# Products over channels: one stream's whole sum, then the other's, in a two-layer diffusion block

## The chip, the cores and the metric

The program runs on one core of a Trainium2 chip. The metric is device time in microseconds (us) of one execution. Engines are named PE (TensorE, matrix products; PEld is its load of the stationary operand), DVE (VectorE), ACT (ScalarE), POOL (GpSimd) and SP (SyncE, which here only issues DMAs).

## The reference, cut to what matters

Two layers act on 512 latent tokens and 256 context tokens, 1024 channels each. Context tokens share all weights. In the last layer only the latent tokens go on behind the mixers. Cut from the reference:

```python
for l in range(DEPTH):                                   # 2 layers
    h_lat = _modulate(_rms_norm(x_lat, norm1_g[l]), m_lat[0], m_lat[1])    # h_ctx likewise
    proj = jnp.concatenate([h_ctx, h_lat], axis=1) @ w_in[l]               # one projection for all mixers
    ya_l = _conformer_conv(a_l, ...)                     # 31 taps over tokens, layer norm, silu
    yb_l = _neighbourhood_attention(qb_l, kb_l, vb_l, kb_c, vb_c, rpb[l], rows)   # 8 heads of 64
    yc_l, yc_c = _gated_deltanet(...)                    # two directions, chunks of 64
    # merge: z = sigmoid(ga)*(ya@w_br[0]) + sigmoid(gb)*(yb@w_br[1]) + sigmoid(gc)*(yc@w_br[2]); z @ w_out
    x_lat = x_lat + m_lat[2][:, None, :] * _merge(mg_l, ya_l, yb_l, yc_l, w_branch[l], w_out[l])
    # feed-forward: (silu(gate) * val) @ w_down, gate and val = 3-tap conv of h @ w_up, 2 x 2816 wide
    x_lat = x_lat + m_lat[5][:, None, :] * _conv_ffn(h2_lat, ffn_up[l], ...)
    # x_ctx the same, in the first layer only
```

## The kernel before

**Operands.** Activations lie channel-major: eight tiles of 128 channels, with 512 columns for the latent stream ("l") and 256 for the context ("c"). Each value is split into a rounded part and the rest, so a stream has tile pairs `hl`/`ol` (latent) and `hc`/`oc` (context). A weight is split the same way in `wunit` (L126 to L133): a DMA on SP's queue brings `raw`, ACT casts it to `whi` (L131), DVE subtracts to get `wlo` (L132). A product over 1024 channels has eight steps k, and in each step three terms: `hl` by `whi`, `ol` by `whi`, `hl` by `wlo` (and the same for the context). So a latent result is a sum of 24 instructions of 512 columns in one PSUM bank, a context result one of 24 instructions of 256 columns in another.

**Two routines issue these products.** `mm_b` (L143 to L154) issues a whole sum at once. It serves the projections before the DeltaNet (`proj_b`, L475; tiles `pjl`, `pjc`), the branch products of the merge (L1281; `mbl`, `mbc`), the output projection (L1321; `wo`, one stream a call), and in the feed-forward the up products (`up_mm`, L1434; `upl`, `upc`) and the down products (L1390; `dn` for both streams). In its loops the streams are innermost: for each k and each term first the latent product, then the context product, so 512 and 256 columns alternate. The first three up units of the first layer call it stream by stream, because the latent half of the normalised input is ready before the context's, and so do the down products of the last part of that layer.

`mm_gen` (L442 to L449) issues the same products as a generator, with the same alternation, and after each k gives a number: the microseconds that it accounts for what it issued, 3 x 768 / 2400 = 0.96 with both streams. Units made from it (the gate projections, whose results `mg_units` turns into `mge` by a tanh on ACT at L1125, and the projections of the convolution, `conv_a_proj`) wait in a queue, with those of the attention's projections (`na`, L584, 0.33 a step) and of the convolution's layer norm.

**What sets the order.** `fill(us)` (L426 to L440) takes the queue's units from the front and steps them until the sum of the numbers that they give has reached `us`:

```python
while us > 0 and (q or self.live):
    if self.live is None:
        self.live = q.popleft()
        ...
    try:
        us -= next(self.live)
```

It is called in the DeltaNet (its chunk products, the block inverse, the scan and its output) and in the attention, with constants for each place and layer: in the first layer `fill(2.1)` behind each step of the attention, and `fill(2.5)` behind each step that prepares its operands. The step that reaches the sum is issued whole. What is left in the queue behind the attention is issued in `finish` (L404). Each unit loads and splits the next unit's weights when it begins. Beneath this, a scheduler of the framework sets the order of instructions on each engine from their dependencies, so the order on PE is not that of the code throughout.

**Stages**, with the starts that the trace shows for the first layer: projections before the DeltaNet (about 99 us), its chunk products (first `kk` at 212), block inverse, scan, the second direction (366), the transposes of its output (`oT`, L1016, last at 508; ACT copies them to `oev`, L1018, and a DMA writes `yc`), the attention's operands (loads `ax`, L1148, transposes `aT`, L1154), its jobs (536 to 698: scores `sc`, softmax on DVE and ACT, transposed probabilities `PT`, L1218, values `yl`/`yc`, L1233) with the convolution's taps (`ca`, L519) on DVE beside them, the rest of the queue (698 to 770), merge, output projection, feed-forward (953 to 1516). The second layer follows with the same stages; its queue's units and everything behind the mixers have one stream only.

Of the kernel before, what the change touches and what calls it, by code (L numbers as in the profile page):

```python
# [64 lines left out]
class Net:  # L65
# [76 lines left out]

    def mm_b(self, outs, w, xs, then={}):  # L143

        n = len(xs[0])
        for k in range(n):
            wk = w(k)
            for i, (a, b) in enumerate(((0, 0), (0, 1), (1, 0))):
                for o, x in zip(outs, xs):
                    self.nc.tensor.matmul(o, wk[a], x[k][b], start=(k == 0 and i == 0), stop=(k == n - 1 and i == 2))  # L150
            if k in then:
                then[k]()

    def pair_tiles(self, s, k):  # L154
        n = NL if s == "l" else NX
# [284 lines left out]
                self.live = None  # L440

    def mm_gen(self, outs, w, xs):  # L442
        n, t = len(xs[0]), sum(o.free_size() for o in outs) * 3 / 2400
        for k in range(n):
            wk = w(k)
            for i, (a, b) in enumerate(((0, 0), (0, 1), (1, 0))):
                for o, x in zip(outs, xs):
                    self.nc.tensor.matmul(o, wk[a], x[k][b], start=(k == 0 and i == 0), stop=(k == n - 1 and i == 2))  # L448
            yield t  # L449

    def proj_gen(self, src, both):
        hi, lo = self.wunit(src, 1024)
# [1078 lines left out]
```

## Time and profile before

| | before |
|---|---|
| median of 3 runs | 2596.06 us (2586.71 to 2603.39) |
| profiled execution | 2594.31 us, its span 2592.5 us |
| busy share of the span | PE 96%, PEld 83%, DVE 71%, ACT 41%, POOL 0% |
| mean granted clock of PE | 0.983 |

The profile is of one execution, which took 2594.31 us; its span, first to last instruction, is 2592.5 us. Busy shares are averages over stages with different limits. A product's row has its own duration; consecutive products overlap, so how fast they are issued is read from the differences of their starts.

### The profile page before, as it was taken

How to read it: one execution, taken by the hardware profiler on the slowest of the kernel's cores; microseconds unless marked ns; L12 is line 12 of the kernel's file. 1: busy time of each engine (PE TensorE's matmuls, PEld its weight loads, DVE VectorE, ACT ScalarE, POOL GpSimd, SP SyncE). 2: the span in 40 equal slices, each digit the busy share in tenths (PEclk: the TensorE clock that was granted, in tenths of full speed). 3: DMA queues.
4: the chain of work that ended last, by engine and by line, in shares of the span. 5: the costliest groups of instructions: out<-in, count | busy, mean ns of one | idle time of the engine just before them, and what ended most of it. 6: DMA issues, size and time to landing. Idle time of an engine off the chain costs nothing. (4 is left out here: it accounts for less than half of the span.)

```text
span 2592.5 us, 42262 instructions
## 1 busy us (share of the span) xinstructions
PE 2494.4 (96%) x16079; PEld 2156.6 (83%) x16079; DVE 1851.6 (71%) x4138; ACT 1067.5 (41%) x2159; POOL 8.4 (0%) x32
## 2 busy tenths in 40 slices
PE   6999999989999999999999999998989999999999
PEld 4889898967778888888888898887877778888887
DVE  6675578789679888776656477776768977755463
ACT  4564343445342244223223355634344543533242
POOL 0000000000000000000000000000000000000000
PEclk9999999999999999999999989998999999999999
DMA  7224434353458554453442342343446376322332
GB/s 253 91 76 137 138 99 140 98 177 109 149 186 270 179 176 125 121 161 115 150 135 87 110 141 95 120 134 112 146 125 211 100 251 188 130 90 98 98 98 90
DMA packets 207276, 356.77 MB, mean 138 GB/s; under 512 B 54832, under 2 KB 103200, under 8 KB 206944
## 3 DMA queue, kind: packets, MB, share of 16 engines
q1 hardware_dynamic: 182176, 320.97, 39.3%
q10 hardware_dynamic: 24896, 33.09, 3.6%
q8 instruction: 127, 2.08, 0.3%
q14 instruction: 77, 0.63, 0.1%
HBM read 297.31 MB, written 56.68 MB: 137 GB/s over the span
## 5 line engine op out<-in xcount | busy, mean ns | idle before, releaser
L132 DVE TENSOR_TENSOR wlo<-raw,whi 128x1024 fp32r<-128x1024 f32 (+2 forms) x319 | 385.4, 1209 | 292.3 <-ACT whi L131 289.1
L131 ACT CAST whi<-raw 128x1024 fp32r<-128x1024 f32 (+2 forms) x319 | 331.8, 1041 | 616.2 <-PE dn L150 197.7
L150 PE MATMUL upl<-hl,whi 128*128 128x512 f32 (+1 forms) x728 | 282.4, 389 | 2.4 <-ACT hl L322 1.9
L150 PE MATMUL upl<-ol,whi 128*128 128x512 f32 (+1 forms) x728 | 282.1, 388 | 0.0
L150 PE MATMUL upl<-hl,wlo 128*128 128x512 f32 (+1 forms) x728 | 280.9, 386 | 0.2 <-DVE wlo L132 0.2
L448 PE MATMUL pjl<-hl,whi 128*128 128x512 f32 x512 | 210.6, 411 | 7.6 <-ACT whi L131 7.6
L519 DVE SCALAR_TENSOR_TENSOR ca<-yp,caw,ca 128x783 f32<-128x783 f32 (+1 forms) x240 | 212.9, 887 | 6.7 <-ACT ca L512 4.6
L448 PE MATMUL pjl<-ol,whi 128*128 128x512 f32 x512 | 206.6, 404 | 0.0
L448 PE MATMUL pjl<-hl,wlo 128*128 128x512 f32 x512 | 206.2, 403 | 0.3 <-DVE wlo L132 0.2
L150 PEld LDWEIGHTS upl<-hl,whi 128*128 128x128 f32 x728 | 137.3, 189 | 30.7 <-ACT hl L322 2.1
L150 PEld LDWEIGHTS upl<-ol,whi 128*128 128x128 f32 x728 | 137.5, 189 | 30.0
L150 PEld LDWEIGHTS upl<-hl,wlo 128*128 128x128 f32 x728 | 137.4, 189 | 30.1 <-DVE wlo L132 0.7
L150 PE MATMUL dn<-fll,whi 128*128 128x512 f32 x352 | 139.0, 395 | 0.0
L150 PE MATMUL dn<-fhl,wlo 128*128 128x512 f32 x352 | 139.0, 395 | 0.0
L150 PE MATMUL dn<-fhl,whi 128*128 128x512 f32 x352 | 138.6, 395 | 0.1
L448 PEld LDWEIGHTS pjl<-hl,whi 128*128 128x128 f32 x512 | 97.8, 191 | 29.5 <-ACT whi L131 9.7
L448 PEld LDWEIGHTS pjl<-hl,wlo 128*128 128x128 f32 x512 | 97.6, 191 | 21.6 <-DVE wlo L132 1.2
L448 PEld LDWEIGHTS pjl<-ol,whi 128*128 128x128 f32 x512 | 98.0, 191 | 18.9 <-issue 0.5
L245 DVE CUSTOM_DVE_ANT_1 aj<-at,crows,par 128x512 f32<-128x512 f32 x128 | 93.1, 747 | 27.7 <-DMA at<-ada_t 16.0
L584 PE MATMUL na<-wlo,hl 128*128 128x256 f32 x384 | 108.9, 284 | 0.6 <-DVE wlo L132 0.6
L584 PE MATMUL na<-whi,hl 128*128 128x256 f32 x384 | 109.1, 285 | 0.0
L584 PE MATMUL na<-whi,ol 128*128 128x256 f32 x384 | 109.1, 284 | 0.0
(405 smaller groups left out, 6450.3 us busy)
## 6 DMA issues: line engine op xcount, KB each, us to landing
raw<-w_b SPq DMA_DIRECT2D x88, 512.0 KB
raw<-f_up SPq DMA_DIRECT2D x88, 512.0 KB
at<-ada_t SPq DMA_DIRECT2D x160, 256.0 KB
raw<-w_o SPq DMA_DIRECT2D x32, 512.0 KB
raw<-f_dn SPq DMA_DIRECT2D x32, 448.0 KB
raw<-w_a SPq DMA_DIRECT2D x24, 512.0 KB
mg<-mge ACTq DMA_DIRECT2D x48, 256.0 KB
raw<-w_br SPq DMA_DIRECT2D x24, 512.0 KB
```

What stands on the lines that cost most here:

```text
L131: self.nc.scalar.copy(hi[:, :n], r[:, :n])
L132: self.split = self.nc.vector.tensor_sub(lo[:, :n], r[:, :n], hi[:, :n]).ins
L150: self.nc.tensor.matmul(o, wk[a], x[k][b], start=(k == 0 and i == 0), stop=(k == n - 1 and i == 2))
L245: V.tensor_tensor_reduce(p, w, self.crows[:, r, 4 * h:4 * h + 4], 1.0, m if h else self.p(l, "adab")[:, t:t + 1], ALU.mult, ALU.add, accum ...
L448: self.nc.tensor.matmul(o, wk[a], x[k][b], start=(k == 0 and i == 0), stop=(k == n - 1 and i == 2))
L519: nc.vector.scalar_tensor_tensor(a, y[:, k:k + n], w[:, 31 * c + k:31 * c + k + 1], a, ALU.mult, ALU.add)
L584: self.nc.tensor.matmul(ps[:, :256], x[k][a], wk[b], start=(k == 0 and j == 0), stop=(k == 7 and j == 2))
```

## The change

`mm_b` puts the stream outermost: all k and all terms of the first stream, then all of the second; what hangs behind a step (`then`) is done in the last stream. `mm_gen` does the same, and gives its number after each k of one stream: 3 x 512 / 2400 = 0.64 for a latent step, 0.32 for a context step. A new routine, `mm_k`, holds the three products of a step, so that all these rows have one line, L154. `fill`, its constants and all callers stay.

```diff
     def mm_b(self, outs, w, xs, then={}):
 
-        n = len(xs[0])
-        for k in range(n):
-            wk = w(k)
-            for i, (a, b) in enumerate(((0, 0), (0, 1), (1, 0))):
-                for o, x in zip(outs, xs):
-                    self.nc.tensor.matmul(o, wk[a], x[k][b], start=(k == 0 and i == 0), stop=(k == n - 1 and i == 2))
-            if k in then:
-                then[k]()
+
+        for s in range(len(xs)):
+            for k in range(len(xs[s])):
+                self.mm_k(outs[s], w(k), xs[s], k)
+                if s == len(xs) - 1 and k in then:
+                    then[k]()
+
+    def mm_k(self, o, wk, x, k):
+        for i, (a, b) in enumerate(((0, 0), (0, 1), (1, 0))):
+            self.nc.tensor.matmul(o, wk[a], x[k][b], start=(k == 0 and i == 0), stop=(k == len(x) - 1 and i == 2))
 
     def mm_gen(self, outs, w, xs):
-        n, t = len(xs[0]), sum(o.free_size() for o in outs) * 3 / 2400
-        for k in range(n):
-            wk = w(k)
-            for i, (a, b) in enumerate(((0, 0), (0, 1), (1, 0))):
-                for o, x in zip(outs, xs):
-                    self.nc.tensor.matmul(o, wk[a], x[k][b], start=(k == 0 and i == 0), stop=(k == n - 1 and i == 2))
-            yield t
+        for o, x in zip(outs, xs):
+            for k in range(len(x)):
+                self.mm_k(o, w(k), x, k)
+                yield o.free_size() * 3 / 2400
```

**PE, an up unit of the first layer.** The program's order of PE before, the start of a unit (buffer numbers count the tiles of the stream, one pair for each k):

```order
L150 MATMUL upl<-hl_9933,whi 128x512
L150 MATMUL upc<-hc_9949,whi 128x256
L150 MATMUL upl<-ol_9934,whi 128x512
L150 MATMUL upc<-oc_9950,whi 128x256
L150 MATMUL upl<-hl_9933,wlo 128x512
L150 MATMUL upc<-hc_9949,wlo 128x256
L150 MATMUL upl<-hl_9935,whi 128x512
```

and of the change, the end of one unit and the start of the next:

```order
L154 MATMUL upc<-hc_10011,whi 128x256
L154 MATMUL upc<-oc_10012,whi 128x256
L154 MATMUL upc<-hc_10011,wlo 128x256
L154 MATMUL upl<-hl_9981,whi 128x512
L154 MATMUL upl<-ol_9982,whi 128x512
L154 MATMUL upl<-hl_9981,wlo 128x512
L154 MATMUL upl<-hl_9983,whi 128x512
```

Where a product of each stream stood in turn, 24 of the latent stream now stand in a row, and 24 of the context behind them.

**PE, where the attention of the first layer begins.** Before, the transposes of q and k (`aT`, four to a tile) stand between products of a gate projection (`pjl`, `pjc`):

```order
L448 MATMUL pjl<-ol_156,whi 128x512
L448 MATMUL pjc<-oc_172,whi 128x256
L1154 MATMUL aT<-kc,ax 128x128 x4
L448 MATMUL pjl<-hl_155,wlo 128x512
L1154 MATMUL aT<-kc,ax 128x128 x4
L448 MATMUL pjc<-hc_171,wlo 128x256
L1154 MATMUL aT<-kc,ax 128x128 x4
L448 MATMUL pjl<-hl_157,whi 128x512
```

and of the change:

```order
L154 MATMUL pjl<-hl_161,whi 128x512
L154 MATMUL pjl<-ol_162,whi 128x512
L154 MATMUL pjl<-hl_161,wlo 128x512
L1153 MATMUL aT<-kc,ax 128x128 x48
L1203 MATMUL sc<-akT,aqT 128x256
L1204 MATMUL sc<-akT,aqT 128x256
```

A latent sum now ends in front of the transposes, and between them and the first scores no product of the queue is left. The same counted over the whole first layer, products of the queue (latent + context of `pjl`/`pjc`, and `na`) in the order of PE:

| between | before | change |
|---|---|---|
| start and first `kk` of the layer | 288 + 288, `na` 123 | 288 + 288, `na` 86 |
| first `kk` and last `oT` | 305 + 305, `na` 741 | 312 + 290, `na` 778 |
| last `oT` and first `PT` | 71 + 70 | 24 + 22 |
| first `PT` and the last values (`yl`, `yc`) | 197 + 198 | 153 + 168 |
| behind the attention | 195 + 195 | 279 + 288 |

In the second layer 42 `na` products stand before the first `kk` and 6 in the change, with the other 36 behind it. Between the `ax` loads and the last bias load of the first layer's attention, SP's queue has 4 weight loads instead of 7; between the same places ACT has 7 casts `whi` instead of 10 and 13 tanh `mge` instead of 20, and DVE 7 splits `wlo` instead of 9 and 79 taps instead of 80.

**ACT, behind the last output transposes of the DeltaNet.** Before, the copies of these transposes (`oev`) with their DMAs end here, and a tanh of a gate projection (`mge`) follows a cast:

```order
L1018 COPY oev<-oT 128x512
L1019 DMA yc<-oev 128x512
L1018 COPY oev<-oT 128x256
L1019 DMA yc<-oev 128x256
L131 CAST whi<-raw 128x1024
L1125 ACTIVATE mge<-pjl 128x512
```

and of the change:

```order
L1017 COPY oev<-oT 128x512
L1018 DMA yc<-oev 128x512
L1124 ACTIVATE mge<-pjl 128x512
L1125 DMA mg<-mge 128x512
L1017 COPY oev<-oT 128x256
L1018 DMA yc<-oev 128x256
```

The tanh of a latent result, and the DMA that writes it, now stand in front of the last copy.

## Rows read from the trace of the kernel before

**Rows 1.** Page, part 1: engine, busy us (share of the span), instructions

```profile
PE 2494.4 (96%) x16079; PEld 2156.6 (83%) x16079; DVE 1851.6 (71%) x4138; ACT 1067.5 (41%) x2159; POOL 8.4 (0%) x32
```

**Rows 2.** Windows: start:end, length, busy and count of each engine, PEclk, DMA share, GB/s

```profile
98.00:194.00 96.00, 96.00 (x582) 83.91 (x581) 75.27 (x193) 65.28 (x199) 0.00 (x0) 1.00 0.22 75
983.00:1447.00 464.00, 463.95 (x2638) 403.51 (x2638) 321.37 (x657) 143.75 (x221) 0.16 (x2) 1.00 0.40 127
```

**Rows 3.** Timeline of PE, alternating up products: start us, duration us, instruction

```profile
1199.89 0.40 PE L150 MATMUL upl<-hl,whi 128*128 128x512 f32 x1
...
1220.03 0.40 PE L150 MATMUL upl<-hl,whi 128*128 128x512 f32 x1
```

**Rows 4.** Timeline of PE, first up units of layer 0, stream by stream

```profile
963.46 0.39 PE L150 MATMUL upl<-hl,wlo 128*128 128x512 f32 x1
...
966.86 0.39 PE L150 MATMUL upl<-hl,whi 128*128 128x512 f32 x1
...
973.61 0.28 PE L150 MATMUL upc<-hc,whi 128*128 128x256 f32 x1
...
982.12 0.28 PE L150 MATMUL upc<-hc,wlo 128*128 128x256 f32 x1
```

**Rows 5.** Timeline of PE, down products of layer 0, alternating, then in sequence

```profile
1252.89 0.39 PE L150 MATMUL dn<-fhl,whi 128*128 128x512 f32 x1
...
1261.21 0.39 PE L150 MATMUL dn<-fhl,whi 128*128 128x512 f32 x1
...
1446.80 0.39 PE L150 MATMUL dn<-fhl,whi 128*128 128x512 f32 x1
...
1451.72 0.39 PE L150 MATMUL dn<-fhl,whi 128*128 128x512 f32 x1
```

**Rows 6.** Groups of PE by form: count | busy, mean ns | idle before, releaser

```profile
L150 PE MATMUL upc<-hc,whi 128*128 128x256 f32 x352 | 99.3, 283 | 0.0
L448 PE MATMUL pjc<-hc,whi 128*128 128x256 f32 x256 | 73.8, 288 | 0.5 <-ACT mge L1125 0.5
L150 PE MATMUL dn<-fhc,whi 128*128 128x256 f32 x176 | 49.4, 281 | 0.0
L150 PE MATMUL pjc<-hc,whi 128*128 128x256 f32 x160 | 45.7, 285 | 0.0
L150 PE MATMUL mbc<-hc,whi 128*128 128x256 f32 x96 | 27.1, 282 | 3.5 <-ACT hc L1269 3.1 <-DVE zc L1290 0.5
```

**Rows 7.** Timeline, last oT to first aT of layer 0 (released by, in brackets)

```profile
507.87 0.28 PE L1016 MATMUL oT<-kc,sgr 128*128 128x128 f32 x1
...
515.99 0.37 ACT L1018 COPY oev<-oT 128x256 f32<-128x256 f32 x1 [2.06 <-DMA yc<-oev]
...
520.10 6.52 SPq L1148 DMA_DIRECT2D ax<-na  x12
...
524.45 0.63 PE L1154 MATMUL aT<-kc,ax 128*128 128x128 f32 x4 [0.41 <-DMA mg<-mge]
```

**Rows 8.** Windows around the attention of layer 0, columns as in rows 2

```profile
508.00:524.00 16.00, 16.00 (x92) 13.66 (x90) 12.99 (x13) 5.91 (x10) 0.00 (x0) 1.00 0.55 176
544.00:548.00 4.00, 0.00 (x0) 0.00 (x0) 0.35 (x1) 0.00 (x0) 0.00 (x0) 0.76 0.98 289
548.00:556.00 8.00, 5.92 (x22) 4.00 (x22) 5.16 (x17) 3.97 (x10) 0.00 (x0) 0.50 0.32 104
560.00:640.00 80.00, 78.74 (x597) 61.95 (x594) 77.00 (x167) 42.95 (x101) 0.41 (x6) 1.00 0.36 115
640.00:680.00 40.00, 39.84 (x265) 31.04 (x262) 38.12 (x78) 17.40 (x42) 0.00 (x0) 1.00 0.21 72
680.00:698.00 18.00, 18.00 (x128) 13.99 (x127) 7.73 (x20) 9.74 (x25) 0.00 (x0) 1.00 0.43 140
```

**Rows 9.** Groups of DVE by form, 560 to 680 us, columns as in rows 6

```profile
L132 DVE TENSOR_TENSOR wlo<-raw,whi 128x1024 fp32r<-128x1024 f32 x6 | 7.3, 1213 | 0.0
```

**Rows 10.** Waits of PE, 1740 to 1790 us: waiter, releaser: us, times, longest

```profile
PE iy L1069 <- DMA Td<-e: 5.3, 3, 3.4
```

## What the change does to the time, predicted

> **What bounds the kernel now.** I read the page first, then the stages by windows, then the rows of single products in time order. Over the whole span TensorE (PE) is busy 96% [rows 1]. In the two kinds of stage that hold most of the products that change, the projections before the DeltaNet and the up products of the feed-forward, it is busy for the whole window, while VectorE (DVE) has room [rows 2]. There a nanosecond per product counts in full. The attention of the first layer is another kind of stage: from 560 to 640 us DVE is busy 77.0 of 80 us and PE 78.7, so both are near their limit; only at its end, from 680 on, does DVE fall to 7.7 of 18 [rows 8]. What fills PE there are products of the gate projections, put between the attention's own small products by `fill`.
>
> **How fast a product is issued.** A busy PE row is not the pace, since rows overlap; the pace is start to start. In alternating order 57 pairs of one 512-column and one 256-column product take 1220.03 - 1199.89 = 20.14 us, 353.3 ns a pair [rows 3]. The before kernel also has the new order in one place, the first three up units of layer 0, with the same tiles: 15 steps of 512 columns take 3.40 us (226.7 ns), 71 steps of 256 columns 8.51 us (119.9 ns) [rows 4]. In sequence a pair would cost 346.6 ns, 6.7 ns less. The down products behave the other way: 24 alternating pairs take 8.32 us, 346.7 ns each, and in sequence, in the last part of layer 0, 21 products of 512 columns take 4.92 us, 234.3 ns [rows 5]; with 119.9 ns for the context that is 354.2 ns, 7.5 ns more. So the pace depends on order and tiles, in both directions.
>
> The Trainium skill would expect nothing from this: "TensorE: Matmul & The Clock Gate", section "Back-to-back issue gap", makes the gap N / 2.4 + 2.5 ns at full clock, whatever stands before. By it a pair is an estimated 215.8 + 109.2 = 325 ns in either order. The trace differs: 353.3 and 346.6 ns [rows 3, 4]; by the rule the pace term below would be nothing, and the time that of the third rival.
>
> **The pace term.** [Rows 6] give the context products of each kind; each counts for one of the three terms of the split, so a kind has three times as many pairs.
> - Up: 3 x 352 = 1056, less the 3 x 24 already in sequence, 984 pairs; 984 x 6.7 ns = 6.6 us, in a stage where PE never waits [rows 2].
> - Projections before the DeltaNet, both layers: 3 x 160 = 480 pairs, 3.2 us, PE again busy throughout [rows 2].
> - Branch products of the merge: 288 pairs, 1.9 us at most; its rows show waits for ACT and DVE [rows 6], so I take half, 1.0 us.
> - Gate and convolution projections issued by `fill`: 3 x 256 = 768 pairs, 5.1 us at most; part of them only covers waits of other work, so half, 2.6 us.
> - Down: of 176 the last 64 are in sequence already; 3 x 112 = 336 pairs x 7.5 ns = 2.5 us lost.
>
> Together a gain of 10.9 us (bounds 8 to 13.5, with all or nothing of the halves and the down loss between 1.7, if the context is a little quicker there, and 2.5).
>
> **The filler term.** `mm_gen` now yields after three products of one stream (0.64 or 0.32 us by its own account) instead of after six (0.96 us). `fill(us)` stops at the first step that reaches its sum, so it overshoots less: fill(2.1) issued 2.88 us of account, and now stops at 2.24 to 2.56. The counts in the order show where that goes. Up to the last output transpose of the DeltaNet (oT) both kernels have issued nearly the same. Between it and the first attention probabilities (PT) stood 71 + 70 products (latent + context), and 24 + 22 now: 47 x 226.7 + 48 x 119.9 ns = 16.4 us less. Through the attention jobs stood 197 + 198, and 153 + 168 now: 44 x 226.7 + 30 x 119.9 = 13.6 us less. Behind the attention 84 + 93 more, 30.2 us, run alone in `finish`. PE's total is the same; the question is only whether the stages they left become shorter.
>
> Before the attention: hardly. Between the last oT (507.87) and the first transpose of q and k (aT, 524.45) the chain is: ACT copies oev, its DMA lands, the pool is given back, the loads of ax go out at 520.10, aT starts [rows 7]. In those 16 us PE was full with filler and DVE with taps [rows 8]; the filler is a cover, not the bound. It now runs out after 24 + 22 products, 8.1 us. I take no saving, so 16.4 us are paid again later. In addition the last oev copy stands behind a tanh (mge) that needs a latent product which ends 8.1 us after the last oT; with that tanh, the copy and its DMA the ax loads go out about 1.3 us later than now. Bounds: from 10 us (aT and the first scores closer together without filler between) to 20.
>
> In the attention jobs: in part. Of 120 us (560 to 680) DVE leaves about 5 [rows 8]. The order moves three gate units past the attention: three weight loads on SP's queue, three casts and seven tanh on ACT, two weight splits (wlo) and one tap of the convolution from DVE's list there. The splits take 1.2 us each [rows 9]; with the tap counted as 1.0, a little under a split, DVE gets 3.4 us shorter; half of its 5 us of waiting may go, 2.4; and the last 18 us, where PE is the bound, lose a fifth of their filler (13.6 of 69 us), 2. That is a saving of 7.8 of 13.6, a loss of 5.8 us. Bounds: 0 (all saved) and 13.6 (none).
>
> In layer 1, 36 products of `na` (4.3 us at 119.9 ns) move from in front of the first kk, where PE is full, behind it, before the block inverse, where PE waits 5.3 us for the DMA of the diagonal blocks [rows 10]. I take 3 us saved (bounds 0 and 4.3). In layer 0 37 products move likewise, but PE waits there for no DMA in the trace, so nothing is counted. Also free: each latent result is complete 24 x 119.9 ns = 2.9 us before its unit ends, so its reader on ACT or DVE can start earlier; where PE never waits this hides. Weight halves are needed earlier (the lo half after two products instead of four), but a unit's split is made a unit ahead and PE's waits for wlo are under a microsecond in all.
>
> **The sum.** The profiled execution took 2594.3 us (span 2592.5), 1.8 below the median 2596.1 of the runs shown. 2594.3 - 10.9 + 16.4 + 1.3 + 5.8 - 3 = 2603.9: **2604 us**, 0.4% above it, which a measurement that tells about 1% from no change would call the same. Its own range, with the bounds above, is 2592 to 2616.
>
> **The rivals.**
> - *The filler was not needed.* If the stages shrink by all that left them, only pace and layer 1 remain: 2594.3 - 10.9 - 3 = 2580 us. For it: PE is busy 78.7 of 80 us in the attention [rows 8]. Against it: DVE at 77.0 of the same 80, and a chain of copies and DMAs in front [rows 7].
> - *The clock falls in the attention*, the rival on the slow side. Behind a stretch in which PE did nothing (544 to 548) the next 8 us ran at 0.50 of the clock, the 1.2 GHz level [rows 8]. With less filler PE is idle before aT for some 8 us and again in each job while DVE works. A microsecond at the half clock does half a microsecond of products. The bound of 1% is 2622, 18 us above my sum, so it decides from about 36 us at half clock; a third of the 138 us from 560 to 698 gives 23 us, 2627. Against it: the remaining filler, 55 us, still falls in every job.
> - *Order makes no pace.* If the 6.7 ns belong to the three first units alone, the gain goes and 2594.3 + 16.4 + 1.3 + 5.8 - 3 = 2615 remains. This is the case of the skill's rule above; the 226.7 and 119.9 ns on the same tiles [rows 4] speak against it.
> - *Faster by over 1%*: 2570 would need the filler free and 10 us more from the chain before the attention; no row shows a wait there that this order removes.
>
> **How the numbers follow.** Forecast 0.50, filler free 0.24, clock 0.14, no pace 0.08, faster by over 1% 0.04. Within 1% (2570 to 2622) fall the forecast, the free filler and most of the third rival, less 0.03 for their upper ends: 0.79. Slower: 0.14 + 0.03 = 0.17. Faster: 0.04. The range reaches from just under the free filler, 2578, to 2622, and leaves out the clock case and the fast one, 0.18.
>
> **What would show it.** Right: the up stage of layer 0 with pairs of 346 to 348 ns and some 6 us shorter; down pairs in sequence near 352 to 354; a gap of PE of about 8 us before the first aT; the attention stage shorter by 5 to 10 us and the stretch after it longer by about 30. Wrong: up products at 234 ns as the down ones are; an attention stage shorter by 14 us or more, or one with several half-clock stretches; a gap elsewhere, as at the first kk, where the cover by `na` is 4.4 us shorter in layer 0.

## The result, and the profile after

The change is slower by 0.6%: 2613.6 us median of 17 runs (2599.57 to 2623.47) against 2595.84 us of the kernel before (2586.71 to 2605.62, 17 runs), ratio 1.006, 95% interval 1.0046 to 1.0073. The forecast was 2604 us, same within 1%, range 2578 to 2622.

The profiled execution of the change took 2620.38 us (span 2618.6), 6.8 above the median, where that of before lay 1.5 below its own. A second profile of the change is of an execution of 2614.61 us (span 2612.8). Part 1 of the page of the change, to be held against [rows 1]:

```profile
PE 2496.2 (95%) x16079; PEld 2166.2 (83%) x16079; DVE 1866.9 (71%) x4138; ACT 1073.5 (41%) x2159; POOL 8.4 (0%) x32
```

PE is busy 1.8 us longer, and the span is 26 us longer: the time lies mostly in waits of PE. The windows say where. First the attention of the first layer (first scores to the first transpose behind it) and the rest of the queue (to the first branch product of the merge), before and after (columns: start:end, length, busy and count of each engine, granted clock, DMA share, GB/s):

```profile
535.70:698.00 162.30, 154.03 (x1078) 119.94 (x1078) 137.19 (x298) 76.82 (x185) 0.41 (x6) 0.97 0.35 114
698.00:770.50 72.50, 70.10 (x411) 60.63 (x409) 42.61 (x127) 23.42 (x44) 0.00 (x0) 1.00 0.69 223
```

```profile
543.70:698.50 154.80, 141.26 (x975) 107.15 (x975) 131.46 (x292) 72.45 (x175) 0.41 (x6) 0.93 0.30 98
698.50:801.10 102.60, 100.14 (x593) 88.24 (x592) 57.02 (x156) 31.26 (x56) 0.00 (x0) 1.00 0.61 199
```

The rest of the queue takes 102.6 us in place of 72.5, with 593 rows of PE in place of 411; the attention becomes 7.5 us shorter for it. Second, the timeline of the change from the last output transpose of the DeltaNet to the first transpose of q and k, which answers to [rows 7]:

```profile
512.55 0.31 PE L1015 MATMUL oT<-kc,sgr 128*128 128x128 f32 x1
...
522.56 0.37 ACT L1017 COPY oev<-oT 128x256 f32<-128x256 f32 x1 [0.98 <-DMA yc<-oev]
...
526.58 5.32 SPq L1147 DMA_DIRECT2D ax<-na  x11
...
531.49 0.87 PE L1153 MATMUL aT<-kc,ax 128*128 128x128 f32 x3 [10.54 <-DMA ax<-na]
```

and the windows of that stretch, cut where the filler ends, with three of the attention behind it, which answer to [rows 8]:

```profile
512.00:521.00 9.00, 8.95 (x54) 7.57 (x51) 3.50 (x5) 3.73 (x7) 0.00 (x0) 1.00 0.42 140
521.00:531.40 10.40, 0.00 (x0) 0.00 (x0) 10.11 (x12) 0.96 (x2) 0.00 (x0) 0.61 0.68 215
560.00:640.00 80.00, 78.75 (x601) 61.50 (x598) 75.61 (x171) 43.19 (x103) 0.41 (x6) 0.99 0.34 109
640.00:680.00 40.00, 35.87 (x239) 27.27 (x237) 36.59 (x73) 16.47 (x41) 0.00 (x0) 1.00 0.15 51
680.00:698.00 18.00, 17.32 (x92) 11.56 (x90) 7.95 (x23) 8.29 (x22) 0.00 (x0) 0.72 0.41 137
```

PE is full until 521 and then does nothing for 10.4 us. The chain that it waits for has not become shorter: last `oT` to `aT` is 18.9 us here, 16.7 in the second profile, 16.6 before.

Third, the pace. An up unit in sequence, and a down unit of the first part, from the timeline of PE:

```profile
1171.39 0.40 PE L154 MATMUL upl<-hl,whi 128*128 128x512 f32 x1
...
1176.86 0.28 PE L154 MATMUL upc<-hc,whi 128*128 128x256 f32 x1
...
1179.73 0.40 PE L154 MATMUL upl<-hl,whi 128*128 128x512 f32 x1
```

```profile
1103.97 0.39 PE L154 MATMUL dn<-fhl,whi 128*128 128x512 f32 x1
...
1108.88 0.28 PE L154 MATMUL dn<-fhc,whi 128*128 128x256 f32 x1
...
1111.34 0.40 PE L154 MATMUL dn<-fhl,whi 128*128 128x512 f32 x1
```

24 latent up products take 5.47 us (227.9 ns), 24 of the context 2.87 us (119.6 ns), a pair 347.5 ns. Of the down products 21 latent ones take 4.91 us (233.8 ns) and 21 of the context 2.46 us (117.1 ns), a pair 351 ns.

The table sets stages side by side, in us, from first start to first start of PE rows of each kernel's profile; each column is one execution. "kk to inverse" and "inverse to chunks" are the first direction of the DeltaNet of the first layer, "oT to scores" runs from the first row of the last group of output transposes to the first scores, "queue" is the window behind the attention shown above. "Layer 1" runs from the start of the projections there (the first `ct`, L829 before) to its first chunk products behind the inverse.

| stage | before | change | change, 2nd | E1 | E3 | E5 | E6 | E7 |
|---|---|---|---|---|---|---|---|---|
| projections to kk | 113.1 | 107.6 | 107.7 | 107.6 | 113.2 | 107.7 | 107.6 | 107.6 |
| kk to inverse | 89.2 | 94.1 | 91.8 | 89.0 | 89.4 | 88.8 | 89.8 | 90.4 |
| inverse to chunks | 22.0 | 26.6 | 24.7 | 26.6 | 23.7 | 26.0 | 24.7 | 26.0 |
| oT to scores | 30.2 | 33.6 | 31.0 | 30.8 | 30.0 | 32.6 | 31.0 | 33.5 |
| attention | 162.3 | 154.8 | 151.9 | 160.1 | 153.7 | 158.7 | 153.2 | 161.2 |
| queue | 72.5 | 102.6 | 103.1 | 73.8 | 89.8 | 75.6 | 96.0 | 85.4 |
| up, 2nd and 3rd part | 254.4 | 250.1 | 250.2 | 250.2 | 254.4 | 250.1 | 250.1 | 250.2 |
| down, 1st and 2nd part | 116.9 | 118.2 | 118.2 | 118.2 | 116.7 | 118.3 | 118.2 | 118.2 |
| layer 1 | 205.1 | 202.5 | 201.2 | 202.7 | 204.3 | 200.9 | 202.3 | 200.2 |

How far may one execution be read? Six profiles have the same filler in the attention, 197 + 198 products: before, E1 and E8 to E11. Their attention takes 162.3, 160.1, 157.8, 155.3, 161.1 and 158.7 us, so a difference of a few us in that row is not a finding. Their queue takes 71.9 to 74.9 us. The profiles of E3 and E6 are the fastest of their twelve executions (2595.01 and 2592.91 us against medians of 2608.76 and 2604.78). Some 6 us of that come at the start of layer 1, far from the filler, where before (first row) PE runs at the lower clock, 1.2 GHz, for 13.7 us, and all others for 10 to 17, but not E6 (second row) and E3:

```profile
1535.90:1549.60 13.70, 13.70 (x67) 13.70 (x66) 6.80 (x18) 4.12 (x8) 0.00 (x0) 0.50 0.21 65
1525.00:1560.00 35.00, 33.87 (x264) 32.56 (x263) 27.84 (x80) 18.21 (x34) 0.00 (x0) 1.00 0.41 130
```

So the columns serve to see where products went, and what a kernel costs is read from the medians and ratios.

### The profile page after: what moved, and what is told of

Read it like the earlier page. It is cut to its first block, busy times and chain, and to the rows that moved or that the text cites. A ratio compares the mean times of both kernels' runs of the same rounds, so it can differ in the third digit from the quotient of the medians.

```text
span 2618.6 us, 42222 instructions
## 1 busy us (share of the span) xinstructions
PE 2496.2 (95%) x16079; PEld 2166.2 (83%) x16079; DVE 1866.9 (71%) x4138; ACT 1073.5 (41%) x2159; POOL 8.4 (0%) x32
## 5 line engine op out<-in xcount | busy, mean ns | idle before, releaser
L154 PE MATMUL pjl<-hl,whi 128*128 128x512 f32 x704 | 286.1, 406 | 4.6 <-ACT whi L131 4.6
L154 PE MATMUL pjl<-hl,wlo 128*128 128x512 f32 x704 | 280.1, 398 | 2.6 <-DVE wlo L132 2.6
L154 PE MATMUL pjl<-ol,whi 128*128 128x512 f32 x704 | 279.7, 397 | 0.0
L154 PE MATMUL upl<-ol,whi 128*128 128x512 f32 (+1 forms) x728 | 278.6, 383 | 0.4 <-DVE ol L325 0.4
L154 PE MATMUL upl<-hl,whi 128*128 128x512 f32 (+1 forms) x728 | 278.0, 383 | 0.3 <-ACT hl L324 0.3
L154 PE MATMUL upl<-hl,wlo 128*128 128x512 f32 (+1 forms) x728 | 278.0, 382 | 0.2 <-DVE wlo L132 0.2
L154 PEld LDWEIGHTS pjl<-hl,whi 128*128 128x128 f32 x704 | 133.6, 190 | 31.5 <-ACT whi L131 6.4
L154 PEld LDWEIGHTS upl<-hl,wlo 128*128 128x128 f32 x728 | 136.7, 188 | 27.6 <-DVE wlo L132 0.7
L154 PEld LDWEIGHTS upl<-ol,whi 128*128 128x128 f32 x728 | 136.8, 188 | 25.7 <-DVE ol L325 0.8
L154 PEld LDWEIGHTS pjl<-hl,wlo 128*128 128x128 f32 x704 | 133.2, 189 | 29.9 <-DVE wlo L132 3.0
L154 PEld LDWEIGHTS upl<-hl,whi 128*128 128x128 f32 x728 | 136.7, 188 | 25.7 <-ACT hl L324 0.5
L154 PEld LDWEIGHTS pjl<-ol,whi 128*128 128x128 f32 x704 | 133.8, 190 | 24.2 <-issue 0.9
L154 PE MATMUL dn<-fhl,wlo 128*128 128x512 f32 x352 | 139.5, 396 | 0.0
L154 PE MATMUL dn<-fll,whi 128*128 128x512 f32 x352 | 139.5, 396 | 0.0
L154 PE MATMUL dn<-fhl,whi 128*128 128x512 f32 x352 | 139.2, 396 | 0.0
L154 PE MATMUL pjc<-hc,whi 128*128 128x256 f32 x416 | 118.9, 286 | 1.2 <-ACT nsq L589 1.2
L154 PE MATMUL pjc<-oc,whi 128*128 128x256 f32 x416 | 118.5, 285 | 0.0
L154 PE MATMUL pjc<-hc,wlo 128*128 128x256 f32 x416 | 118.0, 284 | 0.0
```

## The experiments

**E1: only `mm_b` in sequence.** The change, with `mm_gen` as before:

```diff
     def mm_gen(self, outs, w, xs):
-        for o, x in zip(outs, xs):
-            for k in range(len(x)):
-                self.mm_k(o, w(k), x, k)
-                yield o.free_size() * 3 / 2400
+        n, t = len(xs[0]), sum(o.free_size() for o in outs) * 3 / 2400
+        for k in range(n):
+            ...
+            yield t
```

> Only mm_b runs stream by stream; mm_gen alternates as before, so the filler stands where it stood (195 + 195 products behind the attention), except that 36 to 37 products of na move behind the first kk in each layer, as in the change. Theory (pace and filler are two separate terms): up, projections before the DeltaNet, merge and down give -6.6 -3.2 -1.0 +2.5 = -8.3 us and the moved na in layer 1 some -3, so 2584 to 2588 us, ratio 0.995 to 0.997. Rival (the order makes no pace): 2593 to 2599. Rival (the moved na also costs layer 0 the 4 to 5 us by which the stretch of the first block inverse is longer in the change): 2588 to 2592.

Measured: 2581.37 us, ratio 0.9956 (0.994 to 0.9973), 11.4 us less. That half of the change, alone, is a gain; its ratio lies in the theory's range, its median 3 us below it. The stretch of the first block inverse is 4.6 us longer here too, but the projections in front of it are 5.5 us shorter (4.4 of it the 37 products of `na` that stand behind the first `kk` now): in layer 0 the move costs behind the first `kk` what it saves in front, and the prediction had counted nothing for it.

**E2: only `mm_gen` in sequence.** The change, with `mm_b` as before:

```diff
     def mm_b(self, outs, w, xs, then={}):
-        for s in range(len(xs)):
-            for k in range(len(xs[s])):
-                self.mm_k(outs[s], w(k), xs[s], k)
...
+                for o, x in zip(outs, xs):
+                    self.nc.tensor.matmul(o, wk[a], x[k][b], ...)
```

> Only mm_gen runs stream by stream with its smaller account; mm_b alternates as before. In the order no gate product is left between the last oT and the first PT (before 71 + 70), 153 + 168 stand in the attention and 279 + 288 behind it, as in the change. Theory (the filler that is moved behind the attention is the loss): 30 us more behind the attention, some 4 to 8 saved in front, so 2613 to 2622 us, ratio 1.007 to 1.010, above the change by what mm_b gains. Rival (the loss of the change comes from mm_b): 2592 to 2603.

Measured: 2633.34 us, ratio 1.0152 (1.0125 to 1.018), 39.5 us more: the right half, but 11 us above the top of the expectation. 32 us stand where expected (queue 104.6 us), and the attention, 147.9 us, is 14.4 us shorter, all that left it and more than expected (7 to 14 us, held against the six attentions with the filler of before). The rest is in the second direction of the DeltaNet: its stretch to the block inverse took 84.5 us in place of 75.4, the inverse 24.8 in place of 16.6. In this kernel's order the 24 + 22 products that the change has between the last `oT` and the first `PT` stand ahead of that `oT`: the inverse holds 42 + 34 products of the queue where before it held 9 + 10, and they lengthen it, with PE busy nearly throughout. Its windows, before and E2:

```profile
441.40:458.00 16.60, 11.50 (x355) 10.49 (x355) 12.96 (x16) 6.65 (x15) 0.00 (x0) 0.79 0.69 187
455.70:480.50 24.80, 23.64 (x413) 19.78 (x413) 6.67 (x10) 7.16 (x16) 0.00 (x0) 0.89 0.49 137
```

In front of it PE waits, from 371 to 480 us, waiter and releaser, us, times, longest:

```profile
PE iy L1070 <- DMA Td<-e: 7.5, 1, 7.5
```

Before, the same wait takes 1.4 us. Why that DMA came late there was not followed.

**E3: alternation kept, only the number given in parts.** The kernel before, with

```diff
-            yield t
+                if len(xs) > 1 and i:
+                    yield t * (3 - i) / 3
+            if len(xs) == 1:
+                yield t
```

> The kernel before, with alternating products everywhere; only the number that mm_gen gives comes in parts, 0.64 after two of the three terms and 0.32 after the third, so fill overshoots less. In the order 55 + 55 products stand between the last oT and the first PT (before 71 + 70), 170 + 168 in the attention (before 197 + 198), 238 + 240 behind it (before 195 + 195): 43 + 45 products, 15.1 us, move behind the attention without any new order. Theory (the amount of filler behind the attention costs, not the order): 2605 to 2611 us, ratio 1.0035 to 1.006. Rival (the order in the filler costs: long latent sums in the attention's jobs): 2593 to 2599, no change.

Measured: 2608.76 us, ratio 1.0047 (1.0031 to 1.0064), 12 us more. The streams alternate as before, and the kernel is slower: the amount that `fill` issues in its places is enough for a loss, without the order of streams. The queue behind the attention is 17.3 us longer, the attention 8.6 shorter, oT to scores unchanged though 16 + 15 products left it.

**E4: the change with `fill(2.62)` for both constants.**

```diff
-... x=3.7, pre=2.5, att=2.1),
+... x=3.7, pre=2.62, att=2.62),
```

> The change, with two constants of the first layer raised: fill(2.62) in place of fill(2.5) and fill(2.1). In the order 48 + 46 products stand between the last oT and the first PT, 201 + 216 in the attention, 207 + 216 behind it (before 195 + 195, the change 279 + 288). Theory (pace and filler are separate; with the filler put back only the pace remains): the change's 2613.6 less about 24 us, 2586 to 2593 us, ratio 0.996 to 0.999. Rival (sequential sums fit worse between the attention's own products whatever their amount): 2600 to 2610.

Measured: 2592.64 us, ratio 0.999 (0.9973 to 1.0007). Most of the loss is gone with two constants; the queue takes 77.9 us.

**E5: the change, accounted as before.** `mm_gen` issues stream by stream, and gives 0.96 whenever its account has grown by 0.96:

```diff
-                self.mm_k(o, w(k), x, k)
-                yield o.free_size() * 3 / 2400
+                for i, (a, b) in enumerate(((0, 0), (0, 1), (1, 0))):
+                    self.nc.tensor.matmul(...)
+                    u += o.free_size() / 2400
+                    if u > t * (n + 1) - 0.001:
+                        n += 1
+                        yield t
```

> The change, with mm_gen still stream by stream, but giving 0.96 each time its account has grown by 0.96, as the kernel before gives it. In the order 72 + 70 products stand between the last oT and the first PT (before 71 + 70), 192 + 207 in the attention (197 + 198), 192 + 201 behind it (195 + 195). Theory (the loss of the change comes from fill's overshoot alone, the order in the filler costs nothing): like the kernel in which only mm_b changed, 2578 to 2586 us, ratio 0.993 to 0.997. Rival (long latent sums in the filler cost too): 2588 to 2600, ratio 0.997 or more.

Measured: 2588.01 us, ratio 0.9964 (0.9951 to 0.9978). The ratio lies in the theory's range, the median 2 us above it, at the lower edge of the rival's. The same sequence as in the change, with the filler where it was, is faster than before by 9.4 us. Against the change this is 1.006 / 0.9964, 25 us, the price of the account alone. It does not beat E1, so the sequence within the filler gave nothing that can be seen.

**E6 and E7: the filler taken from one place only.** Both are the change with other constants:

```diff
-... x=3.7, pre=2.5, att=2.1),
+... x=21.0, pre=2.5, att=1.9),      # E6: gap full, attention thin
+... x=3.7, pre=2.5, att=2.62),      # E7: gap thin, attention full
```

> The change, with fill(21.0) ahead of the attention's operands in place of 3.7 and fill(1.9) in its jobs in place of 2.1. In the order 72 + 70 products stand between the last oT and the first PT (as before), only 124 + 144 in the attention (before 197 + 198), 260 + 264 behind it (195 + 195): 23 us moved from the attention behind it, none from the gap in front. Theory of the prediction (some half of what leaves the attention is saved there): about 2583 + 10 = 2590 to 2597 us, ratio 0.998 to 1.001. Rival (the attention shrinks by all that leaves it, as in the kernel in which only mm_gen changed, whose attention became 14.4 us shorter for 13.6 us of products): 2580 to 2587, ratio 0.994 to 0.997.

> The change, with fill(2.62) in the attention's jobs in place of fill(2.1) and nothing else. In the order 24 + 22 products stand between the last oT and the first PT (as in the change; before 71 + 70: 16.4 us less), 210 + 216 in the attention (before 197 + 198), 222 + 240 behind it (195 + 195: 11.5 us more). Theory (what leaves the gap saves nothing there and is paid again elsewhere): 2583 + 11.5 behind, and up to 5 in the attention, 2594 to 2601 us, ratio 0.9995 to 1.002. Rival (the gap closes too, and the attention's share was the loss): 2580 to 2588, ratio 0.994 to 0.997.

Measured: E6 2604.78 us, ratio 1.0026 (1.0009 to 1.0043); E7 2602.76 us, ratio 1.0014 (0.9999 to 1.003). E7's ratio lies in the theory's range, its median 2 us above; E6 lies 8 us above the theory's range, and so refutes the rival the more. For the 23 us that left the attention in E6 the attention became 9.1 us shorter. The windows show what holds it there:

```profile
560.00:640.00 80.00, 77.44 (x564) 59.04 (x563) 76.14 (x166) 42.25 (x100) 0.58 (x6) 1.00 0.33 106
640.00:680.00 40.00, 33.88 (x214) 25.13 (x210) 38.56 (x83) 17.36 (x43) 0.00 (x0) 0.93 0.19 63
```

DVE is busy 114.7 of the 120 us, before 115.1 [rows 8]; PE has room now. So most of what left had only covered DVE's work. The ratios say how much: E6 lies 16 us above E5, whose filler stands where that of before does, so of the 23 us some 7 came back, less than the half that the theory gave (each ratio's interval is some 4 us either way). E7 lies 13 us above E5, with 16.4 us taken out of the gap and 11.5 more behind the attention. In E7 the gap is open, waits of PE from 505 to 560 us:

```profile
PE aT L1153 <- DVE ax L1150: 10.7, 1, 10.7
PE PT L1217 <- DVE P L1210: 7.6, 1, 7.6
```

and in E6, whose gap is full, with the same columns:

```profile
PE PT L1217 <- DVE ls L1209: 7.2, 1, 7.2
PE aT L1153 <- DMA ax<-na: 0.6, 1, 0.6
```

With 24 + 22 products or with 72 + 70, oT to scores takes 33.5 and 31.0 us: taking that filler out shortens nothing. With none at all (E2) it takes 27.9, 2.4 less than before for the 24.5 us that left.

**E8: E1, with the down products alternating.** A second routine `mm_alt` is the old `mm_b`:

```diff
             def down(k0, k1, hid, parts, after=None, late=(), st=None):
...
-                    self.mm_b(ps, ...)
+                    self.mm_alt(ps, ...)
```

> The kernel in which only mm_b changed, with the down products of both streams alternating as before. Theory (down products in sequence are slower, pair 347 against 352 ns): each of the two down stages of layer 0 shorter by 0.4 to 0.9 us than in that kernel, 1.4 to 2.5 us in all, 2578 to 2584 us, which the times alone would not tell from 2581; the trace would show pairs of 347 ns again. Rival (the down pairs take 352 ns in either order next to the other new products): no change in the two stages.

Measured: 2580.12 us, ratio 0.9937 (0.9922 to 0.9953), the fastest of all. The two down stages took 116.7 us together, against 118.2 in E1: 1.5 us, as the theory has it. The rest of the distance to E1 is within the two intervals.

**E9, E10, E11: what sets the pace.** In the trace of the change, products of 512 columns in sequence take 227 ns in the up stages and 234 in the down stages. The moving tiles differ in where the program's allocation puts them in a partition: `hl`, `ol` at byte 23008 and on, 32 past a multiple of 64; `fhl`, `fll` at byte 132480 and on, a multiple of 64. E9 puts 32 bytes in front of the latter, on E1; E10 the same on E8; E11 is E9 with 32 bytes in front of the context's `hc`, `oc` and 32 behind them, which also moves the weight tiles `whi`, `wlo` by 64 bytes and leaves `hl`, `ol` where they were.

```diff
         with self.tc.tile_pool(name=f"ffn{l}", bufs=2) as fp:
+            nc.gpsimd.memset(fp.tile([128, 8], F32, tag="pad", name="pad", bufs=1), 0.0)
     def pair_tiles(self, s, k):                          # E11 only
+        if s == "c" and k == 0 and not hasattr(self, "pad0"):
+            self.pad0 = self.act.tile([128, 8], F32, tag="pad0", name="pad0")
...
+        if s == "c" and k == 7 and not hasattr(self, "pad1"):
+            self.pad1 = self.act.tile([128, 8], F32, tag="pad1", name="pad1")
```

> The kernel in which only mm_b changed, with 32 bytes of padding as the first tile of the feed-forward's pool, so that the moving tiles of the down products (fhl, fll, fhc, flc) start 32 bytes past a multiple of 64, as the tiles hl, ol, hc, oc of the up products do, instead of at one. Theory (the pace of a product in sequence goes by where its moving tile starts: 234 and 117.5 ns at a multiple of 64 bytes, 226.7 and 119.9 ns 32 bytes past one, in the trace of the change): down products of 512 columns at 227 ns, of 256 at 120; 1056 x 7.5 - 528 x 2.4 ns = 6.6 us less, 2575 us, ratio 0.992 to 0.995. Rival (it goes by the stage, its other work or its PSUM): 234 ns as before, 2579 to 2586.

> The kernel with alternating down products and mm_b otherwise in sequence, with the same 32 bytes of padding. Theory (the tile's start also decides what alternating costs): alternating down pairs take 353 ns, as the up pairs did before, instead of 347: the two down stages of layer 0 that alternate become 1.1 us longer each (59.5 instead of 58.4 us), while the down products in sequence go from 234 to 227 ns. Rival (the down pairs alternate at 347 ns for another reason): 58.4 us again.

> The padded kernel in sequence, with the context tiles of the activations (hc, oc, 256 columns) moved to a multiple of 64 bytes and the latent ones (hl, ol, 512 columns) left 32 bytes past one. Theory (256 columns are quicker at a multiple of 64, 512 quicker 32 past one): context products at 117.5 ns instead of 119.9, 2.4 ns x 2592 rows, up to 6.2 us less than the padded kernel, 2569 to 2573 us, ratio 0.989 to 0.993; up stage of layer 0 from 116.7 to 115.9 us. Rival (the 2.4 ns belong to the down stage): no change against the padded kernel.

Measured: E9 2582.57 us, ratio 0.9954 (0.9938 to 0.9971), no gain over E1. Its down products of the first part, timeline of PE:

```profile
1070.56 0.40 PE L154 MATMUL dn<-fhl,whi 128*128 128x512 f32 x1
...
1075.46 0.28 PE L154 MATMUL dn<-fhc,whi 128*128 128x256 f32 x1
...
1077.86 0.39 PE L154 MATMUL dn<-fhl,whi 128*128 128x512 f32 x1
```

21 products in 4.90 us, 233.3 ns, not 227: the theory falls. The 21 of the context behind them did change, but the other way, to 2.40 us, 114.3 ns, where 120 were expected and the change has 117.1; the two stages take 117.2 us together, in E1 118.2. E10, 2582.51 us, ratio 0.9963 (0.9946 to 0.9979), did what was expected for the alternating ones:

```profile
1127.72 0.40 PE L163 MATMUL dn<-fhl,whi 128*128 128x512 f32 x1
...
1133.02 0.40 PE L163 MATMUL dn<-fhl,whi 128*128 128x512 f32 x1
```

15 pairs in 5.30 us, 353.3 ns where they took 346.7 [rows 5], by 32 bytes; the two stages went from 116.7 to 118.7 us. Its down products in sequence stayed at 233 ns, as in E9. So 32 bytes turn the sign of the order: the two down stages take 118.2 us in sequence (E1) and 116.7 alternating (E8), and with the padding 117.2 in sequence (E9) and 118.7 alternating (E10). E11 was slower, 2597.13 us, ratio 1.0019 (1.0003 to 1.0034), and not for the reason it was made for:

```profile
1164.92 0.40 PE L154 MATMUL upl<-hl,whi 128*128 128x512 f32 x1
...
1170.06 0.40 PE L154 MATMUL upl<-ol,whi 128*128 128x512 f32 x1
...
1170.53 0.28 PE L154 MATMUL upc<-hc,whi 128*128 128x256 f32 x1
...
1173.36 0.40 PE L154 MATMUL upl<-hl,whi 128*128 128x512 f32 x1
```

22 steps in 5.14 us, 233.6 ns: the latent up products lost their 227 ns though `hl` and `ol` did not move; the weights did, by 64 bytes. The 24 of the context take 2.83 us, 117.9 ns, near the 117.5 expected, but since the weights moved too it does not show that their own start does it. So for 512 columns it is neither the stage nor the moving tile's start by itself. What fits all these rows is that a product of 512 columns takes 227 ns where moving tile and weights start at the same byte modulo 256 (both 224, in the up stages before E11), and 233 to 234 in the other pairings seen (128 with 224 in the down stages, 160 with 224 in E9, 224 with 32 in E11); modulo 128 fits as well, modulo 64 does not (E9). Products of 256 columns go the other way in the same rows: 119.6 ns at 224 with 224, and 114.3 to 117.9 in the other pairings (E9, the change's down stages, E11 with 0 and 32). No run put the down tiles at the weights' place, so this stays open.

**The change once more**, for a second profile:

> The change once more, for a second profile. Theory (the stages that differ by what moved are the same in each execution): the gap in front of the first aT of the attention near 10 us again, the stretch between the attention and the merge 102 us again, PE pairs as before; and the 4 us by which the stretch from the first kk to the block inverse was longer in the first profile (94 us; 90 us in kernels with the same order there) is of that one execution. Rival: it is 94 us again.

Measured: one execution of 2614.61 us, span 2612.8. The wait in front of the first `aT` is 8.3 us, the queue 103.1, the up and down stages as in the first profile (table). From the first `kk` to the inverse it took 91.8 us, not 94.1 nor 90: half of the 4 us were of the one execution.

## Why the prediction was right

**The filler term** was 16.4 + 1.3 + 5.8 = 23.5 us, and carried the sign. Measured: 25 us, as the ratio of the change to E5, which differs from it in the account alone; E3 shows the same cause without any new order. By its parts: the queue grew by 30.1 us (forecast 30.2). Before the attention nothing was saved, as forecast (E7); the gap in front of the first `aT` was 10.5 and 8.3 us in the two profiles (forecast about 8). The delay of 1.3 us by the later `oev` copy is not shown: that copy starts 10.0 us after the last `oT` in place of 8.1, but in E8 and E10, with the filler of before, it is 10.1 and 10.6, and in the second profile `aT` comes 16.7 us after the last `oT`, hardly later than before. The attention became 7.5 us shorter, 10.4 in the second profile (forecast 7.8, and "5 to 10"), in a stage that varies by 7 us with one and the same filler. The half of DVE's waiting and the fifth of the last 18 us were a guess: it fitted at 13.6 us moved, in part by luck, since it left out the clock (below), and it fails at 23 us (E6).

**The pace term** was 10.9 us. Its up part holds: pairs of 347.5 ns where 346 to 348 were forecast, and the second and third up part 4.3 us shorter, the same in every column of the table with the new order. The down loss was over-sized, 2.5 us forecast and 1.3 measured: the latent products took the 233.8 ns foreseen, but the context ones 117.1, not the 119.9 of the up products; the text had named that case as the lower bound, 1.7. The projections gave less than the 3.2 us forecast: in each layer the stage in front of the first `kk` is 5.4 us shorter, of which the moved `na` are 4.4 and 4.3, so 1.0 and 1.1 remain. The merge, 1.0 forecast, cannot be told from its waits. E1's total, 11.4 us, fits the 8.3 + 3 of these terms together. The gain within `mm_gen`, 2.6 us, is not seen: E5 is 2 us slower than E1 where it should have been that much faster, but within intervals of some 4 us each. The bounds of this term, 8 to 13.5, do not follow from its parts, which give 7.3 to 15.1.

**Layer 1**: 3 us were to come from the moved `na` products. The stage is 2.6 and 3.9 us shorter in the two profiles, 1.1 of it the pace of the projections, so 1.5 to 2.8 us. PE's wait for the diagonal blocks [rows 10] did not shrink; from 1655 to 1790 us it reads in the change

```profile
PE iy L1068 <- DMA Td<-e: 5.9, 3, 3.8
PE na L583 <- DVE wlo L132: 2.5, 1, 2.5
```

and a wait for a weight's split stands beside it that was 0.6 us before. In E1 and E4 to E7, which have the change's order there, the stage takes 200.2 to 204.5 us, so this term is not settled better than that.

**The sum** came out 7 to 10 us low, 2604 against 2613.6 by the median and 2611 by the ratio, inside the range. The sum's own range, 2592 to 2616, is narrower than its bounds added up, some 2586 to 2620; the measurement lies in both. By E5, 4.5 us of that are pace and layer 1 that did not come (13.9 forecast, 9.4 measured), 1.5 the filler, and some 1.5 to 1.8 the distance of the profiled execution of before from the median. The rival with free filler is refuted by E3 and E5.

**The clock rival came in part**, and the sum had no term for it. The granted clock over the attention is 0.93, before 0.97. These are the stretches at the lower level, 1.2 GHz, from the last `oT` to the merge: three in the change (rows 1 to 3), three in its second profile (4 to 6), one before (the last).

```profile
523.40:537.00 13.60, 5.45 (x24) 4.84 (x24) 13.22 (x17) 2.54 (x4) 0.00 (x0) 0.50 0.83 287
550.70:560.90 10.20, 7.62 (x36) 5.45 (x37) 7.78 (x23) 4.97 (x12) 0.00 (x0) 0.50 0.19 53
680.40:690.60 10.20, 9.53 (x47) 6.21 (x47) 6.88 (x20) 5.45 (x15) 0.00 (x0) 0.50 0.36 126
523.80:534.00 10.20, 4.48 (x20) 4.11 (x21) 9.83 (x13) 2.40 (x4) 0.00 (x0) 0.50 0.73 247
547.70:557.90 10.20, 6.57 (x31) 4.73 (x33) 7.32 (x22) 4.28 (x10) 0.00 (x0) 0.50 0.21 58
677.40:680.80 3.40, 3.40 (x20) 2.42 (x19) 3.40 (x12) 2.60 (x8) 0.00 (x0) 0.50 0.57 177
546.10:556.30 10.20, 6.22 (x24) 4.24 (x26) 5.66 (x18) 3.97 (x10) 0.00 (x0) 0.50 0.43 143
```

PE is busy 22.6, 14.5 and 6.2 us in them. If half of such a time is lost, an estimate and an upper bound where PE waits for other engines anyway, that is some 8 and 4 us more than before. The last stretch lies in the last 18 us, where PE is nearly always busy (17.3 us), and there the two profiles differ by 6.1 us of busy time and their attentions by 2.9. The executions say the same: in the 17 of the change the mean granted clock has a median of 0.979, in the 29 of before that were run beside E1 0.984, and in the change the fastest (2599.57) has 0.982 and the slowest (2623.47) 0.976. So a part of the 25 us is the clock. No run separates it from the waits: E5 puts the filler back and closes the idle time with it. As a rival for the whole, a median of 2622 us or more, it did not come.

The third rival, a pace that order does not change, is refuted by the rows of the pace in both directions, but it hangs on where the tiles lie: with the weights 64 bytes on (E11), an up pair in sequence takes 351.5 ns (233.6 + 117.9); what an alternating pair takes there was not run. The Trainium skill's rule on it ("TensorE: Matmul & The Clock Gate", section "Back-to-back issue gap", N / 2.4 + 2.5 ns) gives an estimated 325 ns for a pair; the trace does not agree, with 347.5 and 351. That section gives the rule for a matmul in isolation, and says that in a stream of weight loads and matmuls both set the spacing; "whatever stands before" was the prediction's reading.

## What to carry to other kernels

Where a generator's steps feed a budget that stops at the first step past its sum, the size of the step is part of the budget: a change of its grain moves work between stages, and the budget has to be set anew with it (E4, E5). Before work that fills a wait is moved, ask what its stage waits for; here the filler over a chain of copies and DMAs saved next to nothing when it went and cost its whole length elsewhere (E7), and the filler beside a nearly full DVE gave back some 7 of 23 us (E6). Here the order of `mm_b` alone, with the `na` that it moves, was worth 11 us (E1); leaving the down products alternating gave 1.5 us more in their stages (E8). One profile of one execution did not tell stages apart that differ by a few us: the attention varied by 7 us with the same filler.

## What the runs showed of the hardware that was not expected

Start to start, a product of 512 columns in sequence takes 226.7 or 234 ns and one of 256 columns 119.9, 117 or 114, at full granted clock, with nothing changed but the bytes at which its operands start: 64 bytes more for the weights took the latent up products from 227 to 233.6 ns (E11), and 32 bytes more for the moving tiles the context's down products from 117.1 to 114.3 (E9). The price of alternating 512 and 256 columns depends on them too: 346.7 ns a pair and 353.3 with the moving tiles 32 bytes on (E10). So the sign of this change's pace term belongs to the placement, not to the order as such: over the two down stages sequence costs 1.5 us (E1 against E8), and with 32 bytes of padding it saves 1.5 (E9 against E10). Which positions go together was not found.
